# Differential values of all heads in 512-column products over four tiles of tokens, behind head 1's projections

## The chip, the cores and the metric

The kernel runs on one core of a Trainium2 chip. Five engines matter: TensorE (PE; its weight loads are shown apart as PEld) multiplies 128x128 blocks and writes only into PSUM; VectorE (DVE) and ScalarE (ACT) read PSUM and do the element work; GpSimd (POOL) does a few small steps and issues some transfers; SyncE (SP) issues most transfers. Each engine works through its own queue in order, and the engines wait for one another by semaphores. The metric is the device time of one execution in microseconds, the median of several.

## The reference

Two layers over 512 tokens of 1024 channels. Each layer normalises its input, projects it with one large matrix `w_in`, and feeds three token mixers (differential attention, a convolution module, neighbourhood attention), whose outputs are gated, merged and followed by a feed-forward block and a gated input embedding. The change touches the values of the differential attention, and one buffer of the neighbourhood attention:

```python
proj = h @ w_in[i]
qa, ka, va, glu_in, qc, kc, vc, gates = jnp.split(proj, SPLITS, axis=-1)
ya = diff_attention(qa, ka, va, ...)
...
v = va.reshape(B, S, HA, DV_A).transpose(0, 2, 1, 3)
...
a = jax.nn.softmax(s, axis=-1)
a = (a[:, :, 0] - lam * a[:, :, 1]).astype(v.dtype)
return jnp.einsum('bhqk,bhkd->bhqd', a, v)
```

There are four differential heads with values 128 wide, so `va` is 512 tokens by 512 columns. The neighbourhood attention has eight heads of 64, and its values `vc` are 512 by 512 too.

## The kernel before

Every operand of a product is split into a high and a low part, and a product is made of three matmuls (high by high, high by low, low by high) that add up in one PSUM bank. Activations lie with their channels on the partitions: `self.h` holds eight chunks of 128 channels by 512 tokens. A projection (`proj`, `gemm`) loads one block of weights of 128x1024, splits it on ACT and DVE, and makes 8 x 3 matmuls of 512 columns into a bank. `weights` issues the load and the split ahead of their place, by a priority; the loads go through SP's queue.

The order of TensorE's instructions is written by hand (`manual_schedule`): it is the order of the program text. The other engines' orders are laid out by a scheduler from priorities and readiness. PSUM has eight banks, handed out by tag: three "mm", two "sc", two "tr", one "av" (`pbufs`, line 297). A bank goes back to its tag when its last reader is done.

`layer` (line 428) lays out a layer: the convolution's gated input, the neighbourhood attention's projections of four pairs of heads (`natten_in`) and its values (`natten_v`), then the differential attention's projections of four heads (`diff_in`, each a query and a key) and its values, gates, output products and merging. Within this foreground the attention itself runs as units, generators that are put in a queue (`later`) with a delay and a gap: `chunk` counts the foreground's groups of matmuls, and every fourth call is a tick (`tick`), at which waiting units go on by one step and the next unit of the queue may start. So a unit's step stands at a fixed number of chunks, whatever the foreground then is.

A neighbourhood unit (`natten_unit`, line 695) takes two "sc" banks for its two 128x256 scores (`scores`, line 807; matmuls at L811), each read by one DVE operation that also takes a bias tile loaded from memory (load at L702, operation at L710); two ticks later it transposes the probabilities into "tr" banks, and two ticks after that it sums the values (L753, L754) into "av" for a pair's first head and into "mm" for its second (line 748). A differential unit (`diff_unit`, line 844) calls `probs` (line 892): twice a 128x512 score into an "sc" bank, a maximum on DVE (L902), and an exponential on ACT that reads the bank again (its instruction is recorded at the helper's line, L143). Every second unit goes on with transposes (L859) and value sums.

`diff_in` also takes the head's query and key through a rotation: a copy to "rp", four small transfers on SP's queue (L829), additions and products on DVE, a split, and small transfers that stack the parts (L660): four for the query, eight for the key.

`natten_v` (line 663) makes the neighbourhood values for all heads at once: four accumulators, one for each tile of 128 tokens, of 512 columns each (L676 to L678), in two "mm" banks, "av" and "sc". `diff_v` (line 840) makes the differential values in two calls for two heads each by `values` (line 599): two "mm" banks, each with two tiles of 256 columns (L615 to L619). The first call stands behind head 0's projections, the second behind head 2's. `_vblocks` lays out its weights. Both end in the split of the values on ACT and DVE.

## Time and profile before

| | |
|---|---|
| median of 3 runs | 1776.03 us |
| lowest and highest run | 1776.01 and 1777.37 us |
| span of the profiled execution | 1776.7 us |
| PE busy | 1767.5 us, 99% of the span |
| DVE busy | 1421.7 us, 80% |
| ACT busy | 894.4 us, 50% |
| POOL busy | 103.0 us, 6% |

The profile shows one execution; the runs give no other time for it than its span. A row of the timeline has its start in microseconds from the start of the span, the duration, the engine, the line of the kernel, the operation with what it writes and reads, and in brackets the idle time before it with the work that ended it. Matmuls overlap in the pipeline, so that the distance of two starts, not the duration, is what one costs. A row of waits has the engine and tile that waited, the one waited for, the microseconds in total, the count and the longest. A row of a stretch of time has the busy time and count of each engine in the order PE, PEld, DVE, ACT, POOL, then TensorE's granted clock (1.00 is full speed), the share of the transfer engines and GB/s.

### The profile page before, as it was taken

The page shows a single profiled execution, that of the slowest core. Times are in us where ns is not written, and L with a number is a line of the kernel's source. Part 1 is how long each engine was busy: PE and PEld are TensorE (multiplying, and loading weights), DVE is VectorE, ACT ScalarE, POOL GpSimd, SP SyncE. Part 2 cuts the span into 40 slices and gives each one's busy share as a digit, 9 for nine tenths or more (in the row PEclk, how much of TensorE's full clock was granted, in tenths as well). Part 3 has the DMA queues.
Part 4 walks back from the last instruction along what each step waited for, and adds up shares of the span by engine and source line. Part 5 has one row for each costly group of instructions (what it writes and reads, how often), then busy time and mean ns, then how long its engine had stood idle before and what let it go on. Part 6 is the DMA issues. An engine that isn't in the chain of part 4 may idle for free.

```text
span 1776.7 us, 27451 instructions
## 1 busy us (share of the span) xinstructions
PE 1767.5 (99%) x10210; PEld 1559.6 (88%) x10210; DVE 1421.7 (80%) x2418; ACT 894.4 (50%) x1561; POOL 103.0 (6%) x146
## 2 busy tenths in 40 slices
PE   9999999999999999999999999999999999999998
PEld 7888888888899899998888888888888998989987
DVE  7878887998798587787776788889887976867776
ACT  5577555225565254454545765452356643534454
POOL 0000000000111010100000000000001110101000
PEclk9999999999999999999999999999999999999999
DMA  5666641334757366543447655423357664655332
GB/s 202 188 186 176 161 125 42 113 98 140 230 150 193 109 167 160 132 131 123 145 124 198 176 165 149 113 71 95 93 179 198 171 179 115 173 144 151 98 108 92
DMA packets 113509, 256.07 MB, mean 144 GB/s; under 512 B 14560, under 2 KB 19424, under 8 KB 113376
## 3 DMA queue, kind: packets, MB, share of 16 engines
q1 hardware_dynamic: 99984, 229.93, 42.3%
q0 software_dynamic: 12672, 23.07, 8.3%
q8 instruction: 81, 1.33, 0.3%
q10 hardware_dynamic: 720, 1.31, 0.2%
q14 instruction: 52, 0.43, 0.1%
HBM read 215.46 MB, written 7.34 MB: 125 GB/s over the span
## 4 chain that ended last, share of the span: by engine, by line
PE 96%; DVE 2%; ACT 1%; issue 0%; DMA 0%; POOL 0%; ACTq 0%; POOLq 0%; DVEq 0%
PE ffn_mm L1017 4%; PE ffn_mm L1019 4%; PE ffn_mm L177 4%; PE ffn_mm L179 4%; PE ffn_mm L178 4%; PE ffn_mm L1018 4%; PE ffn_sc L1019 3%; PE ffn_sc L1017 3%; PE ffn_sc L1018 3%; PE mergea_mm L177 2%; PE mergea_mm L178 2%; PE mergea_mm L179 2%; PE diff_sc L811 2%; PE gatec_mm L177 2%; PE gatec_mm L178 2%; PE gatec_mm L179 2%
## 5 line engine op out<-in xcount | busy, mean ns | idle before, releaser
L160 DVE SCALAR_TENSOR_TENSOR conv_z<-glu_z,pre_par,conv_z 128x512 f32<-128x512 f32 x240 | 179.4, 748 | 3.3
L143 ACT ACTIVATE ffn_wh<-ffn_wr 128x1024 fp32r<-128x1024 f32 (+1 forms) x92 | 92.7, 1014 | 111.7 <-PE ffn_mm L178 77.1
L987 POOL DMA_DIRECT2D ffn_qk<-w_fu x88 | 78.0, 990 | 605.7 <-DMA ffn_qk<-w_fu 414.7
L157 DVE TENSOR_TENSOR ffn_wl<-ffn_wr,ffn_wh 128x1024 fp32r<-128x1024 f32 (+1 forms) x92 | 107.4, 1173 | 5.4 <-ACT ffn_wh L143 4.9
L157 DVE TENSOR_TENSOR ffn_t<-ffn_mm,wo_rb 128x512 f32<-128x512 f32 (+1 forms) x64 | 38.6, 604 | 67.9 <-PE ffn_mm L179 67.8
L143 ACT ACTIVATE mergea_wh<-mergea_wr 128x1024 fp32r<-128x1024 f32 (+1 forms) x32 | 27.1, 846 | 96.8 <-PE mergea_mm L178 79.6
L143 ACT ACTIVATE ffn_wh<-ffn_qk 128x1024 fp32r<-128x1024 f32 x44 | 46.7, 1060 | 35.9 <-PE ffn_mm L178 15.7
L157 DVE TENSOR_TENSOR ffn_wl<-ffn_qk,ffn_wh 128x1024 fp32r<-128x1024 f32 x44 | 53.8, 1224 | 11.3 <-ACT ffn_wh L143 11.3
L157 DVE TENSOR_TENSOR ffn_t<-ffn_t,ffn_t 128x512 f32<-128x512 f32 (+1 forms) x46 | 31.3, 680 | 31.4 <-ACT ffn_t L143 30.9
L143 ACT ACTIVATE diff_a<-diff_sc,diff_s 128x512 f32<-128x512 f32 x32 | 22.0, 686 | 61.0 <-DVE diff_s L902 61.0
L177 PE MATMUL ffn_mm<-ffn_v,ffn_wh 128*128 128x512 f32 x132 | 51.4, 389 | 0.0
L178 PE MATMUL ffn_mm<-ffn_v,ffn_wh 128*128 128x512 f32 x132 | 51.4, 389 | 0.0
L179 PE MATMUL ffn_mm<-ffn_v,ffn_wl 128*128 128x512 f32 x132 | 51.3, 389 | 0.0
L177 PE MATMUL ffn_mm<-ffn_y,ffn_wh 128*128 128x512 f32 x132 | 51.3, 389 | 0.0
L178 PE MATMUL ffn_mm<-ffn_y,ffn_wh 128*128 128x512 f32 x132 | 51.3, 389 | 0.0
L179 PE MATMUL ffn_mm<-ffn_y,ffn_wl 128*128 128x512 f32 x132 | 51.3, 389 | 0.0
L1019 PE MATMUL ffn_mm<-wo_h,ffn_wl 128*128 128x256 f32 x176 | 49.8, 283 | 0.0
L1019 PE MATMUL ffn_sc<-wo_h,ffn_wl 128*128 128x256 f32 x176 | 49.8, 283 | 0.0
L1018 PE MATMUL ffn_mm<-wo_h,ffn_wh 128*128 128x256 f32 x176 | 49.8, 283 | 0.0
L1018 PE MATMUL ffn_sc<-wo_h,ffn_wh 128*128 128x256 f32 x176 | 49.8, 283 | 0.0
L1017 PE MATMUL ffn_sc<-wo_h,ffn_wh 128*128 128x256 f32 x176 | 49.8, 283 | 0.0
L1017 PE MATMUL ffn_mm<-wo_h,ffn_wh 128*128 128x256 f32 x176 | 49.8, 283 | 0.0
(876 smaller groups left out, 6588.6 us busy)
## 6 DMA issues: line engine op xcount, KB each, us to landing
ffn_qk<-w_fu POOLq DMA_DIRECT2D x88, 256.0 KB, 5.7
ffn_wr<-w_fg SPq DMA_DIRECT2D x44, 512.0 KB, 3.7
ffn_wr<-w_fd SPq DMA_DIRECT2D x32, 448.0 KB, 3.9
ffn_r<-w_fu SPq DMA_DIRECT2D x44, 256.0 KB, 3.7
ffn_qk<-w_fg SPq DMA_DIRECT2D x44, 256.0 KB, 4.3
ffn_qk<-w_fu SPq DMA_DIRECT2D x44, 256.0 KB, 4.6
natten_wr<-w_in SPq DMA_DIRECT2D x16, 512.0 KB, 4.3
natten_b<-bias SPq DMA_DIRECT2D x32, 256.0 KB, 4.0
```

The lines of the kernel that those rows point to most:

```text
L143: i = self.nc.scalar.activation(out, in_, func, **kw)
L157: return self.nc.vector.tensor_tensor(out, a, b, op)
L160: return self.nc.vector.scalar_tensor_tensor(out, a, s, b, op0, op1)
L177: mm(out, wh, ah, start=first, stop=False)
L178: mm(out, wh, al, start=False, stop=False)
L179: mm(out, wl, ah, start=False, stop=last)
L811: self.nc.tensor.matmul(out, st4[:, u, qs], st[:, ks], start=n == 0, stop=n == 1)
L987: nc.gpsimd.dma_start(q, wu[:, lo], accum_op=ALU.add)
L1017: mm(out, wh[:, c], bh, start=first and k == 0, stop=False, skip_group_check=True)
L1018: mm(out, wh[:, c], bl, start=False, stop=False, skip_group_check=True)
L1019: mm(out, wl[:, c], bh, start=False, stop=k == 3, skip_group_check=True)
```

## The change

The wide loop of `natten_v` becomes a function of its own, `wide_values`, and the differential values use it: one call for all four heads, in 512-column products over four tiles of tokens, with the accumulators in the three "mm" banks and one "sc" bank. The call stands behind head 1's projections; the second call, behind head 2's, is gone. The neighbourhood sums of the last pair of heads take the "av" bank for both heads. The weights are laid out like the neighbourhood values'.

```diff
@@ layer
         self.diff_in(0, sd, ya)
-        self.diff_v(0, sd)
         self.diff_in(1, sd, ya)
+        self.diff_v(sd)
         self.gate_c(acc, 0)
         self.diff_in(2, sd, ya)
-        self.diff_v(1, sd)
         self.diff_in(3, sd, ya)
@@
-    def values(self, ap, parts):
+    def wide_values(self, ap, tags):
 
         mm = self.nc.tensor.matmul
-        accs = [self.ps("mm", (P, 2, 256)) for _ in range(2)]
-        for o in range(0, KD, 4):
-            wh, wl = self.weights(ap[:, o * 256:(o + 4) * 256], 1024)
...
+        accs = [self.ps(t) for t in tags]
+        for o in range(0, KD, 2):
+            wh, wl = self.weights(ap[:, o * 512:(o + 2) * 512], 1024)
+            self.background(self.low, self.bg["values"] if self.phase == "natten" else 0)
+            for k in (o, o + 1):
+                s = slice((k - o) * 512, (k - o + 1) * 512)
+                for t, out in enumerate(accs):
+                    hi, lo = (a[:, t * P:(t + 1) * P] for a in self.halves(self.h[k]))
+                    mm(out, hi, wh[:, s], start=k == 0, stop=False)
+                    mm(out, hi, wl[:, s], start=False, stop=False)
+                    mm(out, lo, wh[:, s], start=False, stop=k == KD - 1)
                     self.chunk()
...
+        return accs
@@ natten_v
-        accs = [self.ps(t) for t in ("mm", "mm", "av", "sc")]
...
+        accs = self.wide_values(self.a["w_vc"][self.i], ("mm", "mm", "av", "sc"))
@@ natten_unit
-        av = self.ps(("av", "mm")[u], (P, 256))
+        av = self.ps("av" if pr == 3 else ("av", "mm")[u], (P, 256))
@@
-    def diff_v(self, g, st):
+    def diff_v(self, st):
         self.phase = "diff"
-        st["v", g] = self.values(self.a["w_va"][self.i, g], lambda v, a: ((v[:, 0:256], v[:, 256:512], a),))
+        accs = self.wide_values(self.a["w_va"][self.i], ("mm", "mm", "mm", "sc"))
+        for g in range(2):
+            st["v", g] = [self.sb("v", [P, 2, 512], F32R) for _ in range(2)]
+            for t, acc in enumerate(accs):
+                v = st["v", g][t // 2][:, t % 2]
+                self.split(v[:, 0:256], v[:, 256:512], acc[:, g * 256:(g + 1) * 256])
@@ _layout
-        "w_va": _vblocks(w_in[:, :, OFF_VA:OFF_VA + 512]),
+        "w_va": _wide(w_in[:, :, OFF_VA:OFF_VA + 512]),
```

More of the change, by code (lines that the diff above doesn't have):

```diff
@@ L597, in conv @@
         yield from self.norm(st[0], CB, (3, 1), done)
-    def values(self, ap, parts):
+    def wide_values(self, ap, tags):
         mm = self.nc.tensor.matmul
-        accs = [self.ps("mm", (P, 2, 256)) for _ in range(2)]
-        for o in range(0, KD, 4):
-            wh, wl = self.weights(ap[:, o * 256:(o + 4) * 256], 1024)
-            both = [(k, t) for k in range(o, o + 4) for t in range(4)]
-            if o == 0:
-                both.sort(key=lambda kt: kt[1] // 2)
-            for n, (k, t) in enumerate(both):
-                s = slice((k - o) * 256, (k - o + 1) * 256)
-                out = accs[t // 2][:, t % 2, :]
-                ts = slice(t * P, (t + 1) * P)
-                mm(out, self.h[k][:, 0, ts], wh[:, s], start=k == 0 and t % 2 == 0,
-                   stop=False, skip_group_check=True)
-                mm(out, self.h[k][:, 0, ts], wl[:, s], start=False, stop=False,
-                   skip_group_check=True)
-                mm(out, self.h[k][:, 1, ts], wh[:, s], start=False,
-                   stop=k == KD - 1 and t % 2 == 1, skip_group_check=True)
-                if n % 2:
-                    self.chunk()
-        vs = []
-        for acc in accs:
-            v = self.sb("v", [P, 2, 512], F32R)
-            for t in range(2):
-                for hi, lo, a in parts(v[:, t], acc[:, t]):
-                    self.split(hi, lo, a)
-            vs.append(v)
-        return vs
+        accs = [self.ps(t) for t in tags]
[9 more added lines that the diff above has]
+                    mm(out, lo, wh[:, s], start=False, stop=k == KD - 1)
+                    self.chunk()
+        return accs
     def natten_in(self, pr, st, ys):
@@ L666, in natten_v @@
         self.phase = "natten"
-        mm = self.nc.tensor.matmul
-        accs = [self.ps(t) for t in ("mm", "mm", "av", "sc")]
-        for o in range(0, KD, 2):
-            wh, wl = self.weights(self.a["w_vc"][self.i][:, o * 512:(o + 2) * 512], 1024)
-            self.background(self.low, self.bg["values"])
-            for k in (o, o + 1):
-                s = slice((k - o) * 512, (k - o + 1) * 512)
-                for t, out in enumerate(accs):
-                    hi, lo = (a[:, t * P:(t + 1) * P] for a in self.halves(self.h[k]))
-                    mm(out, hi, wh[:, s], start=k == 0, stop=False)
-                    mm(out, hi, wl[:, s], start=False, stop=False)
-                    mm(out, lo, wh[:, s], start=False, stop=k == KD - 1)
-                    self.chunk()
+        accs = self.wide_values(self.a["w_vc"][self.i], ("mm", "mm", "av", "sc"))
         vs = [[self.sb("v", [P, 2, 512], F32R) for _ in range(2)] for _ in range(2)]
@@ L1359, in _blocks @@
     return np.ascontiguousarray(w).reshape(*lead, m // P, P, (k // P) * P)
-def _vblocks(w):
-    w = w.reshape(L, KD, P, 2, 256).transpose(0, 3, 2, 1, 4)
-    return np.ascontiguousarray(w).reshape(L, 2, P, KD * 256)
 def _wide(w):
```

## The prediction

> **What bounds the kernel now.** I read the busy line first, then the chain of waits, then the waits of TensorE, to see whether a TensorE microsecond is a microsecond of the kernel.

> ```profile
> PE 1767.5 (99%) x10210; PEld 1559.6 (88%) x10210; DVE 1421.7 (80%) x2418; ACT 894.4 (50%) x1561; POOL 103.0 (6%) x146
> PE 96%; DVE 2%; ACT 1%; issue 0%; DMA 0%; POOL 0%; ACTq 0%; POOLq 0%; DVEq 0%
> PE pre_av L325 <- DVE pre_zeror L398: 1.1, 1, 1.1
> PE natten_tr L734 <- ACT natten_e L143: 0.3, 2, 0.2
> PE natten_tr L736 <- ACT natten_e L143: 0.3, 2, 0.2
> PE natten_tr L736 <- DVE natten_a L157: 0.2, 1, 0.2
> ```

> PE is on 96% of the chain and waits for other engines 1.9 us in all. So the kernel is as long as PE's instruction stream: fewer PE cycles come off the span, and a new PE wait goes on it in full, since there is no idle time that it could replace. DVE and ACT have slack; what matters of them is how soon they empty a PSUM bank that PE wants.

> **The products themselves.** Per layer, `values` runs twice, 2 x 8 x 4 x 3 = 192 products of 256 columns; `wide_values` runs 8 x 4 x 3 = 96 of 512. Durations in the rows overlap, so the price is the distance of starts. First and last of 24 narrow ones, and of 9 wide ones (the neighbourhood values, the same loop):

> ```profile
> 198.72 0.28 PE L615 MATMUL diff_mm<-diff_wh,glu_h 128*128 128x256 f32 x1
> ...
> 201.48 0.28 PE L619 MATMUL diff_mm<-diff_wh,glu_h 128*128 128x256 f32 x1
> ```
> ```profile
> 70.20 0.39 PE L676 MATMUL natten_mm<-natten_wh,glu_h 128*128 128x512 f32 x1
> ...
> 72.02 0.39 PE L678 MATMUL natten_sc<-natten_wh,glu_h 128*128 128x512 f32 x1
> ```

> 2.76 / 23 = 0.120 us against 1.82 / 8 = 0.2275 us. Per layer 192 x 0.120 - 96 x 0.2275 = 23.0 - 21.8 = 1.2 us; two layers: **-2.4 us**. [...] Weight loads (4 of 1024 columns a layer), their splits and the eight evacuating splits keep their number and size: nothing.

> **What moves.** Both versions call the chunk counter 32 times a layer for these values, so the attention units, which start at fixed ticks (four chunks), keep their ticks while the projections around them change. Counting ticks from a layer's first neighbourhood projection: head 0 ends at 32 and head 1, now next, at 36; the values fill 36 to 44. The units there are: neighbourhood scores of the last unit (pair 3, second half, second head) at 37; neighbourhood sums of pair 3 at 38, 39, 40, 41; head 0's scores at 39, 41, 43 and 45. The rows of before fit this count: head 0's first scores come inside head 1's k projection, the second in gate_c, the third in head 2's q.

> During 36 to 44 the accumulators hold all three "mm" banks and one of the two "sc" banks. Every unit that asks for two "sc" banks now gets one, and PE, in order, stands until it is read. Behind the waiting matmul stand the remaining value products, gate_c and everything later; ACT and DVE then wait for those.

> **Head 0's scores.** `probs` makes two 128x512 scores (u = 0, 1). With one bank, u = 1 starts when the reduction and the exponential of u = 0 are done. First, second and third `probs` of layer 1:

> ```profile
> 172.32 0.48 PE L811 MATMUL diff_sc<-diff_qk 128*128 128x512 f32 x1
> 172.86 0.39 PE L811 MATMUL diff_sc<-diff_qk 128*128 128x512 f32 x1
> 174.31 1.28 DVE L902 TENSOR_REDUCE diff_s<-diff_sc 128x1 f32<-128x512 f32 x2
> 175.02 0.69 ACT L143 ACTIVATE diff_a<-diff_sc,diff_s 128x512 f32<-128x512 f32 x1 [1.80 <-DVE diff_s L902]
> ...
> 180.49 0.40 PE L811 MATMUL diff_sc<-diff_qk 128*128 128x512 f32 x1
> 182.73 0.69 ACT L143 ACTIVATE diff_a<-diff_sc,diff_s 128x512 f32<-128x512 f32 x1 [2.19 <-DVE diff_s L902]
> ...
> 186.88 0.39 PE L811 MATMUL diff_sc<-diff_qk 128*128 128x512 f32 x1
> 187.07 0.69 DVE L902 TENSOR_REDUCE diff_s<-diff_sc 128x1 f32<-128x512 f32 x1
> 187.86 0.69 ACT L143 ACTIVATE diff_a<-diff_sc,diff_s 128x512 f32<-128x512 f32 x1 [2.24 <-DVE diff_s L902]
> ```

> From the start u = 1 has now to the end of u = 0's exponential: 175.71 - 172.86 = 2.85, 183.42 - 180.49 = 2.93, 188.55 - 186.88 = 1.67 us. The third has DVE free at once (0.69 reduction, 0.69 exponential and the product's tail), so 1.67 is the floor. In the first two DVE first empties neighbourhood tiles, work that comes at the same ticks afterwards. Per layer from 3 x 1.67 = 5.0 to 2.85 + 2.93 + 1.67 = 7.5; I take 6.5, since the waiting itself lets DVE catch up somewhat: **+13.0 us** (10.0 to 15.0).

> [...]

> **The last neighbourhood scores.** Two 128x256 scores, each read by one DVE operation that also needs the bias tile:

> ```profile
> 163.68 0.36 PE L811 MATMUL natten_sc<-natten_qk 128*128 128x256 f32 x1
> ...
> 164.00 0.28 PE L811 MATMUL natten_sc<-natten_qk 128*128 128x256 f32 x1
> ```
> ```profile
> 164.60 1.85 SPq L702 DMA_DIRECT2D natten_b<-bias  x1
> ```
> ```profile
> 169.32 0.42 DVE L710 CUSTOM_DVE_ANT_0 natten_b<-natten_sc,natten_b 128x256 f32<-128x256 f32 x1
> ```

> The second score wants its bank at 164.00 and would get it at 169.74: 5.7 us, because this bias was issued late, behind the key and query stacks of head 0 on SP's queue. That is the upper bound. The lower is a bias already there: product tail (0.28) and DVE (0.42), 0.7 us. Head 1's 20 small transfers (8 rotations, 12 stacks) are moved forward on the same queue, but a bias is issued ahead by priority; between ends far apart I take the middle, 3.2 us: **+6.4 us** (1.4 to 11.4).

> **One "av" bank for four sums.** Sums of the second head used an "mm" bank:

> ```profile
> 167.47 0.23 PE L754 MATMUL natten_av<-natten_a,natten_x 128*128 128x128 f32 x1
> ...
> 170.84 0.64 PE L753 MATMUL natten_mm<-natten_pt,natten_v 128*128 128x256 f32 x4
> ```
> ```profile
> 171.13 0.42 DVE L157 TENSOR_TENSOR natten_y<-natten_y,natten_av 64x256 fp32r<-64x256 f32 x1
> ```

> The next sum starts at 170.84 and the bank would be free at 171.55: 0.7 us late, where DVE had been held by the bias above. Twice a layer, 0 to 0.7 each; I take 0.4 a layer: **+0.8 us** (0 to 2.8).

> **The ends of the values.** At the start the fourth accumulator takes an "sc" bank of the neighbourhood scores just before; nine products (2.05 us) cover it. At the end `gate_c` wants an "mm" bank and head 0's fourth scores the second "sc" bank. The same evacuation after the neighbourhood values ends with

> ```profile
> 76.69 0.41 DVE L157 TENSOR_TENSOR natten_v<-natten_sc,natten_v 128x256 fp32r<-128x256 f32 x1
> ```

> 77.10, or 5.1 us after the last product starts at 72.02. Until the fourth scores' u = 1 pass the product (0.23), eight transposes (0.8), twelve products of gate_c (2.7) and u = 0 (0.5), 4.2 us: 0.9 us short if DVE does that bank last. I take 0.6 a layer for both ends together: **+1.2 us** (0 to 3).

> **Sum.** -2.4 + 13.0 + 6.4 + 0.8 + 1.2 = +19.0 us on the profiled execution's span of 1776.7; its span lies 0.7 above the median of the runs, 1776.03, so **1795 us**. All low ends: -2.4 + 10.0 + 1.4 = +9.0, 1785.0. All high ends: -2.4 + 15.0 + 11.4 + 2.8 + 3.0 = +29.8, 1805.8.

> **Rivals.** *The banks come free in time (not slower).* Then only the shorter products are left: 1776.0 - 2.4 = 1773.6 us. It decides if the scores' bank is not held, that is if the units leave the ticks of the values. For it: bank waits on PE are absent from the table today. Against: at these ticks each unit takes two of two "sc" banks, and even the best row leaves 1.67 us.

> *Head 1's chain becomes the bound.* The rotary chains of heads 0 and 1 now follow each other with no values between. Their buffers ("rp", four) are held until the stacks are sent, and SP sends in order:

> ```profile
> 159.50 1.14 SPq L660 DMA_DIRECT2D diff_qk<-diff_kh  x2
> ...
> 163.26 1.24 SPq L660 DMA_DIRECT2D diff_x<-diff_rp  x2
> ```

> Head 0's k stacks end at 164.5, while head 1's k projection will end near 160 and wants one of these buffers to leave its "mm" bank. If it has to wait for them, the third accumulator waits some 4.5 us, twice: 1795 + 9 = 1804 us. Against: a rotated copy's buffer is freed earlier, by the addition.

> *The clock falls in the wait.* Near the end PE has no work after 1769.7:

> ```profile
> 1770.00:1774.00 4.00, 0.00 (x0) 0.00 (x0) 1.35 (x4) 0.71 (x2) 0.65 (x1) 1.00 0.66 244
> 1774.00:1774.50 0.50, 0.00 (x0) 0.00 (x0) 0.00 (x0) 0.00 (x0) 0.00 (x0) 1.00 0.41 143
> 1774.50:1775.00 0.50, 0.00 (x0) 0.00 (x0) 0.00 (x0) 0.00 (x0) 0.00 (x0) 0.73 0.06 20
> ```

> The granted clock stays 1.00 for about 5 us and then halves. Only a neighbourhood wait at its upper bound (5.7) is that long. At half clock for as long as the wait, PE loses 2.9 us a layer on top of the 5.7: 1795 + 2 x (5.7 - 3.2 + 2.9) = 1806 us. [...]

> **How the numbers follow.** Bank waits as summed: 0.80; banks free in time: 0.08; head 1's chain: 0.07; clock: 0.05. A measurement of this kernel can tell no less than about 0.2% (3.6 us) from no change, so 1773.6 would read as the same; faster needs 1.2 us more than the products give, 0.03. Same: 0.06, the rest of that rival and a little from partial waits. Slower: 0.91. The range reaches from 1784, just under all low ends, to 1806, all high ends and both slower rivals; left out are the first rival and small remainders.

> **What would show it.** Right: PE waits for ACT `diff_a` before three of L811's matmuls in each layer, 1.7 to 2.9 us each, and once for DVE L710; wide products 0.2275 us apart; PE's busy time down by about 2.4 us; no wait before the fourth scores above 1 us. Wrong: those three waits missing, or a largest wait at the first value products (head 1's chain), or a granted clock under 1.00 between the values. The prediction is wrong in size if the neighbourhood wait is outside 0.7 to 5.7 us, and wrong in kind if the span falls.

## The result and the profile after

| | before | after |
|---|---|---|
| median, lowest to highest | 1776.7 us, 1776.01 to 1778.1 (4 runs beside the changed kernel) | 1824.13 us, 1821.48 to 1825.63 (4 runs) |
| span of the profiled execution | 1776.7 us | 1823.0 us |
| PE busy, instructions | 1767.5 us, 10210 | 1779.3 us, 10018 |
| waits of PE for other engines, summed | 1.9 us | 38.1 us |
| mean granted clock of TensorE | 0.999 | 0.993 |

The ratio is 1.0265 (95% interval 1.0251 to 1.0280): slower by 47 us, where 19 were forecast and 30 was the upper end. The busy line of the page after, and the line of its chain by engine:

```profile
PE 1779.3 (98%) x10018; PEld 1554.1 (85%) x10018; DVE 1423.0 (78%) x2418; ACT 900.8 (49%) x1561; POOL 102.9 (6%) x146
PE 89%; DVE 5%; DMA 3%; ACT 2%; issue 1%; SPq 0%; POOL 0%; ACTq 0%; DVEq 0%; POOLq 0%
```

192 matmuls fewer, as counted, and yet 11.8 us more PE busy time: some matmuls must have become slower. PE's share of the chain falls from 96% to 89%; what it lost went to DVE, transfers and ACT. The table of PE's waits, which had four rows before (engine, line and tile that waited, the one waited for, microseconds, count, longest), now reads:

```profile
PE diff_sc L782 <- ACT diff_a L143: 10.1, 5, 2.8
PE natten_sc L782 <- DVE natten_s L681: 8.8, 2, 5.0
PE diff_mm L609 <- ACT diff_rp L143: 4.4, 2, 2.2
PE diff_tr L835 <- DVE diff_t L157: 3.2, 2, 1.6
PE diff_sc L782 <- DMA diff_qk<-diff_rp: 2.8, 1, 2.8
PE diff_sc L782 <- DVE diff_v L157: 2.4, 2, 1.2
...
PE natten_av L724 <- DVE natten_y L157: 1.3, 2, 0.7
...
PE gatec_mm L177 <- DVE diff_v L157: 0.9, 2, 0.4
```

(Lines 782, 609, 835 and 681 are the matmuls of the scores, of the wide products and of the differential transposes, and the reduction of the neighbourhood scores.) The waits are 36.2 us longer. The longest ones of layer 1 in order of time:

```profile
163.94 0.50 PE L609 MATMUL diff_mm<-diff_wh,glu_h 128*128 128x512 f32 x1 [2.21 <-ACT diff_rp L143]
...
171.35 0.58 PE L782 MATMUL natten_sc<-natten_qk 128*128 128x256 f32 x1 [3.87 <-DVE natten_s L681]
...
185.48 0.79 PE L782 MATMUL diff_sc<-diff_qk 128*128 128x512 f32 x1 [2.80 <-DMA diff_qk<-diff_rp]
197.12 0.50 PE L782 MATMUL diff_sc<-diff_qk 128*128 128x512 f32 x1 [2.01 <-ACT diff_a L143]
205.46 0.50 PE L782 MATMUL diff_sc<-diff_qk 128*128 128x512 f32 x1 [1.65 <-ACT diff_a L143]
```

The first is the first product of the third accumulator of the values: its "mm" bank still holds head 1's k projection. ACT's copy that frees it starts at 163.29, with no idle time of ACT from 158.81 up to it, and before the last stacks of head 0 are sent:

```profile
163.29 0.60 ACT L143 ACTIVATE diff_rp<-diff_mm 128x512 f32<-128x512 f32 x1
```
```profile
163.42 1.18 SPq L643 DMA_DIRECT2D diff_qk<-diff_rp  x2
```

The second is the last neighbourhood unit, the other three are head 0's first three `probs`, each waiting for its single "sc" bank. (At 185.48 the record names a transfer; the same matmul of layer 2 waits 2.80 us for ACT `diff_a`, and it is the bank here too: ACT's exponential of the first score runs from 184.65 to 185.34.)

The other part is the clock. The stretches of layer 2 around the neighbourhood wait, which there lasts from 1070.32 to 1075.29 (the granted clock is the number behind the five engines' busy times):

```profile
1073.00:1076.40 3.40, 1.11 (x4) 1.01 (x5) 0.71 (x3) 0.60 (x2) 0.00 (x0) 0.50 0.39 117
1076.40:1079.75 3.35, 3.35 (x10) 2.58 (x9) 2.55 (x7) 1.52 (x4) 0.00 (x0) 0.50 0.38 87
1079.75:1083.00 3.25, 3.25 (x21) 2.86 (x20) 1.67 (x3) 2.32 (x4) 0.00 (x0) 1.00 0.33 76
```

Half clock from 1073 on, while PE still waits, and through the next 4.5 us of work. In layer 1 the wide products show what it does to each:

```profile
172.37 0.63 PE L610 MATMUL diff_mm<-diff_wl,glu_h 128*128 128x512 f32 x1
172.80 0.63 PE L611 MATMUL diff_mm<-diff_wh,glu_h 128*128 128x512 f32 x1
...
191.66 0.40 PE L609 MATMUL diff_mm<-diff_wh,glu_h 128*128 128x512 f32 x1
191.89 0.39 PE L610 MATMUL diff_mm<-diff_wl,glu_h 128*128 128x512 f32 x1
```

0.43 us from start to start at half clock against 0.23 at full. The clock was at half from 165.00 to 175.24 and from 185.48 to 188.89 in layer 1, from 1072.94 to 1079.77 and from 1090.01 to 1093.42 in layer 2. Without the waits inside, PE worked 17.7 us there, and would have taken half of it at full clock: 8.8 us lost.

**The account** of the profiled execution: waits +36.2, clock +8.8, products -2.4 as priced, together +42.6; measured +46.3. The remaining 3.7 us over 23 new waits are 0.16 us each. An edge that the list leaves out has that size: idle time is counted from a matmul's modelled end (0.39 us after its start), while the next would have started 0.23 us after it. That it is this edge is not shown: in the place-alone kernel below the same sum leaves nothing over, and the spans of the kernel before differ by 2.7 us from execution to execution (1774.1 to 1776.8 us in thirteen later ones), the profiled one being among the longest.

### The profile page after: what moved, and what is told of

The parts are those of the page before. It is cut to its first block, busy times and chain, and to the rows that moved or that the text cites. A ratio compares the mean times of both kernels' runs of the same rounds, so it can differ in the third digit from the quotient of the medians.

```text
span 1823.0 us, 27073 instructions
## 1 busy us (share of the span) xinstructions
PE 1779.3 (98%) x10018; PEld 1554.1 (85%) x10018; DVE 1423.0 (78%) x2418; ACT 900.8 (49%) x1561; POOL 102.9 (6%) x146
## 4 chain that ended last, share of the span: by engine, by line
PE 89%; DVE 5%; DMA 3%; ACT 2%; issue 1%; SPq 0%; POOL 0%; ACTq 0%; DVEq 0%; POOLq 0%
PE ffn_mm L993 4%; PE ffn_mm L995 4%; PE ffn_mm L177 4%; PE ffn_mm L178 4%; PE ffn_mm L179 4%; PE ffn_mm L994 4%; PE ffn_sc L995 3%; PE ffn_sc L994 3%; PE ffn_sc L993 3%; PE mergea_mm L178 2%; PE mergea_mm L177 2%; PE mergea_mm L179 2%; PE gateb_mm L178 2%; PE gateb_mm L177 2%; PE wo_mm L177 2%; PE gateb_mm L179 2%
## 5 line engine op out<-in xcount | busy, mean ns | idle before, releaser
L143 ACT ACTIVATE ffn_wh<-ffn_wr 128x1024 fp32r<-128x1024 f32 (+1 forms) x92 | 92.8, 1015 | 111.9 <-PE ffn_mm L178 79.0
L157 DVE TENSOR_TENSOR ffn_wl<-ffn_wr,ffn_wh 128x1024 fp32r<-128x1024 f32 (+1 forms) x92 | 107.4, 1173 | 5.6 <-ACT ffn_wh L143 5.0
L157 DVE TENSOR_TENSOR ffn_t<-ffn_mm,wo_rb 128x512 f32<-128x512 f32 (+1 forms) x64 | 38.7, 605 | 68.1 <-PE ffn_mm L179 68.1
L143 ACT ACTIVATE mergea_wh<-mergea_wr 128x1024 fp32r<-128x1024 f32 (+1 forms) x32 | 27.1, 848 | 96.8 <-PE mergea_mm L178 79.4
L878 DVE TENSOR_REDUCE diff_s<-diff_sc 128x1 f32<-128x512 f32 x64 | 43.2, 687 | 29.3 <-PE diff_sc L782 29.2
L143 ACT ACTIVATE ffn_wh<-ffn_qk 128x1024 fp32r<-128x1024 f32 x44 | 46.7, 1061 | 36.6 <-PE ffn_mm L178 15.9
L157 DVE TENSOR_TENSOR ffn_wl<-ffn_qk,ffn_wh 128x1024 fp32r<-128x1024 f32 x44 | 53.8, 1224 | 10.7 <-ACT ffn_wh L143 10.7
L157 DVE TENSOR_TENSOR ffn_t<-ffn_t,ffn_t 128x512 f32<-128x512 f32 (+1 forms) x46 | 31.3, 680 | 31.9 <-ACT ffn_t L143 31.4
```

What stands on the lines that cost most here:

```text
L143: i = self.nc.scalar.activation(out, in_, func, **kw)
L157: return self.nc.vector.tensor_tensor(out, a, b, op)
L878: nc.vector.tensor_reduce(out=m[:, u:u + 1], in_=sc, op=ALU.max, axis=AX.X, negate=True)
```

## The experiments

The ratios are against runs of the kernel before on the same chip. A kernel without a ratio was timed in a single execution, beside 1777.05 us of the kernel before; what its trace shows carries it.

### Which part costs it: place, banks, width

*Width.* The changed kernel, with every 512-column product of the differential values made as two of 256:

```diff
-                    mm(out, hi, wh[:, s], start=k == 0, stop=False)
...
+                    for g in range(1 if self.phase == "natten" else 2):
...
+                        mm(out[:, q], hi, wh[:, c], start=k == g == 0, stop=False, skip_group_check=True)
```

> The changed kernel with its place and its four accumulators, but products of 256 columns (two for each of 512). If the loss is all in the banks and the place: the changed kernel's 1824 us and 2.4 us more, 1824 to 1829 us, the same waits of L782, and 2.4 us more of product time. If the wide products themselves bring on part of the loss (longer groups, later evacuation): below 1820 us.

1827.03 us, ratio 1.0282 (1.0267 to 1.0298). The loss stays; the products' share is 2.9 us by the medians, near the forecast 2.4, though the two kernels' intervals overlap and their waits differ too (36.8 us in sum here, 38.1 in the changed kernel).

*Place.* The kernel before, with both its narrow calls behind head 1, in two "mm" banks as ever:

```diff
         self.diff_in(0, sd, ya)
-        self.diff_v(0, sd)
         self.diff_in(1, sd, ya)
+        self.diff_v(0, sd)
+        self.diff_v(1, sd)
         self.gate_c(acc, 0)
         self.diff_in(2, sd, ya)
-        self.diff_v(1, sd)
         self.diff_in(3, sd, ya)
```

> The kernel before with its narrow products, but both calls behind head 1's projections; each call holds two mm banks and no sc bank. Theory of bank waits: the place alone costs only the later start of heads 2 and 3 (the wait of the transposes, L859 here, for a tr bank, 3.2 us in the changed kernel) and small change, 1778 to 1783 us; no wait of L811 for diff_a, no fall of the clock. Rival (the rotation chains of heads 0 and 1 side by side are the loss): waits of PE for diff_rp and diff_qk as in the changed kernel and 1790 us or more.

1799.59 us, ratio 1.0127 (1.0112 to 1.0142), with no accumulator in an "sc" bank and the sums' banks untouched: 23 us for the place alone. The time is the rival's, but not by the waits that it named: PE's waits in this kernel are 17.5 us, none of them for a copy to `diff_rp`, and none for a bank of head 0's scores:

```profile
PE natten_tr L734 <- DVE natten_pt L157: 6.2, 2, 3.1
PE natten_sc L811 <- DVE natten_s L710: 4.4, 4, 1.2
PE diff_tr L859 <- DVE diff_t L157: 3.2, 2, 1.6
```

The first of them in DVE's timeline, and the matmul that it lets go:

```profile
173.81 0.69 DVE L157 TENSOR_TENSOR diff_rp<-diff_rp,diff_kh 128x512 fp32r<-128x512 f32 x1
...
176.21 0.68 DVE L157 TENSOR_TENSOR diff_rp<-diff_rp,diff_r 128x512 f32<-128x512 f32 x1
176.92 0.69 DVE L157 TENSOR_TENSOR natten_pt<-natten_tr,natten_pt 128x512 fp32r<-128x512 f32 x1
```
```profile
177.76 0.30 PE L734 MATMUL natten_tr<-pre_ident,natten_e 128*128 128x128 f32 x1 [3.10 <-DVE natten_pt L157]
```

DVE never stands idle between these rows. It works through head 1's rotation, and the operation that empties the transposes' bank has its turn behind it. In the kernel before, the values stood between the two heads' projections and gave PE work while DVE rotated. With 15.6 us more waits and three falls of the clock (by the reckoning above 4.9 us) the sum is 20.5 us, and this span is 20.3 us longer. So the 47 us go, along these steps, to the place (1776.5 to 1799.6), to the four held banks and the sums' single bank (1799.6 to 1827.0, 27 us), less the 3 of the wider products.

*One "av" bank alone.* The kernel before with only that edit:

```diff
-        av = self.ps(("av", "mm")[u], (P, 256))
+        av = self.ps("av" if pr == 3 else ("av", "mm")[u], (P, 256))
```

> The kernel before with one edit alone: the neighbourhood sums of the last pair of heads take the av bank for both heads. The prediction's term: two waits of PE a layer of 0 to 0.7 us for the bank, 0 to 2.8 us in all, 1776.5 to 1779.5 us; the waits of natten_av for natten_y were 1.3 us in the changed kernel. If the edit matters more there: over 1780 us.

1779.46 us, ratio 1.0016 (1.0006 to 1.0025). Two waits a layer, where the prediction had counted the bank as late by 0.7 us twice at most:

```profile
171.08 0.71 PE L753 MATMUL natten_av<-natten_pt,natten_v 128*128 128x256 f32 x4 [0.70 <-ACT natten_e L143]
180.23 0.71 PE L753 MATMUL natten_av<-natten_pt,natten_v 128*128 128x256 f32 x4 [0.79 <-DVE natten_y L157]
```

PE's waits rise from 1.9 to 4.7 us and the time by 2.9 us: these short waits cost their length, and the mean clock stayed at 1.00. The price was right at its upper end.

### Which units pay, and can they be moved out of the way

*Head 0's scores behind the values.* In the changed kernel head 0's units start five ticks later:

```diff
-            self.later(self.diff_unit(head, qt, st4, k2, st, box, ys), 6 if head else 7, 2)
+            self.later(self.diff_unit(head, qt, st4, k2, st, box, ys), 6 if head else 12, 2)
```

> The changed kernel, with head 0's units starting 12 ticks after its projections instead of 7, so that none of its scores stands between the value products; the last neighbourhood scores and sums still do. Theory (waits for a bank, each followed by a spell of half clock): the waits of L782 for diff_a (12.9 us with the one put down to a transfer), the two for the second score bank (2.4 us) and the second fall of the clock in each layer (3.2 us of half clock each, 1.6 us of time) are gone: about 1824 - 12.9 - 2.4 - 3.2 = 1805 us, with the neighbourhood wait (3.9 and 5.0 us) and the first fall unchanged. Rival (ACT, DVE and SP are late because the chains of heads 0 and 1 follow each other, and PE waits for them somewhere anyway): the waits turn up at other places, 1815 us or more.

1843.8 us. The scores' waits fell from 12.9 to 3.5 us, so the held "sc" bank was their cause. But the total rose by 20:

```profile
PE diff_tr L227 <- DVE diff_pt L157: 16.7, 4, 6.1
...
PE diff_tr L227 <- POOL diff_rc L223: 6.8, 2, 3.4
```

The late units now hold "tr" banks that the normalisations need. The waits for the held bank can't be had back this way; of the total it says only that the rival's time, 1815 us or more, came.

*The values behind the first gate product*, so that head 1's chain has that much more time, and head 0's units two ticks later:

```diff
-        self.diff_v(sd)
         self.gate_c(acc, 0)
+        self.diff_v(sd)
...
-            self.later(self.diff_unit(head, qt, st4, k2, st, box, ys), 6 if head else 7, 2)
+            self.later(self.diff_unit(head, qt, st4, k2, st, box, ys), 6 if head else 9, 2)
```

> The changed kernel, with the values one gate projection later (two ticks) and head 0's units two ticks later too, so that three of its scores still fall between the value products, but the last neighbourhood scores and head 1's last copy do not. Theory of bank waits: the neighbourhood wait (8.8 us), the wait for head 1's copy (4.4 us) and the first fall of the clock (about 5 us of time in both layers) are gone, the scores' waits of 10 to 13 us stay: about 1824 - 18 = 1806 us. Rival (the chains of heads 0 and 1 are late): the gate's bank or the scores wait for them instead, 1815 us or more.

1829.26 us. The neighbourhood's wait for its scores and the wait for `diff_rp` are gone, and one of 10 us a layer has come; here it is with the transfers and the work of DVE and ACT ahead of it:

```profile
174.43 2.72 SPq L800 DMA_DIRECT2D diff_rp<-diff_rp  x4
```
```profile
179.99 0.69 DVE L157 TENSOR_TENSOR diff_rp<-diff_rp,diff_r 128x512 f32<-128x512 f32 x1 [3.71 <-DMA diff_rp<-diff_rp]
```
```profile
182.70 0.63 ACT L143 ACTIVATE diff_kh<-diff_rp 128x512 fp32r<-128x512 f32 x1 [5.48 <-DVE diff_rp L157]
183.24 0.58 ACT L143 ACTIVATE gatec_x<-gatec_mm 128x512 f32<-128x512 f32 x1
```
```profile
183.87 0.79 PE L609 MATMUL diff_mm<-diff_wh,glu_h 128*128 128x512 f32 x1 [10.01 <-ACT gatec_x L143]
```

The gate's bank was ready to be read, but ACT, in order, stood 5.5 us at head 1's split for DVE; DVE had stood 3.7 us for the rotated parts, whose transfers left SP's queue only from 174.43. Head 1's chain is late whoever comes next.

*A bias buffer from another set for the last neighbourhood unit*, so that its load need not wait for an earlier unit's tile:

```diff
-        b = self.sb("b", [P, 2, NW])
+        b = self.sb("t" if (pr, half, u) == (3, 1, 1) else "b", [P, 2, NW])
```

> The changed kernel, with the bias of the last neighbourhood unit in a buffer of its own, so that its load need not wait for an earlier unit. If the long neighbourhood wait is the bias transfer: it shrinks from 3.9 and 5.0 us to 0.7 to 1.2 us each, and the clock is half for a shorter time after it, about 1824 - 7 - 3 = 1814 us. If it is DVE's own backlog: it stays above 3 us and the time at 1822 to 1826 us.

1819.3 us, between the two forecasts. The neighbourhood wait fell from 8.8 to 3.9 us and that for `diff_rp` from 4.4 to 2.1; 3.3 us came up for `natten_e`, and the scores' stayed at 12.9. The bias was about half of that wait; the other half is the shared bank with DVE's queue ahead of it. PE's waits shrank by 6.0 us in sum, the span by 5.5 (the changed kernel's own four spans differ by 4.1).

*The neighbourhood's tail and heads 2 and 3's units one tick earlier*, in the place-alone kernel and in the changed one:

```diff
-            self.later(self.natten_unit(pr, n // 2, n % 2, st4, k2, st, ys[pr]), 6 if pr == 3 else 5 if pr else 10, 1)
+            self.later(self.natten_unit(pr, n // 2, n % 2, st4, k2, st, ys[pr]), 4 if pr == 3 else 5 if pr else 10, 1)
...
-            self.later(self.diff_unit(head, qt, st4, k2, st, box, ys), 6 if head else 7, 2)
+            self.later(self.diff_unit(head, qt, st4, k2, st, box, ys), (7, 6, 5, 5)[head], 2)
```

> The kernel before with both narrow calls behind head 1 (1799.6 us without further edits), and pair 3's neighbourhood units due four instead of six ticks behind their pair (the queue lets them start one tick earlier), heads 2 and 3's units five instead of six. If the place costs time because the tail of the neighbourhood meets head 1's rotary chain on VectorE and SyncE: the waits for natten_s and natten_pt (12 us), for diff_t (3.2) and the three clock falls (about 5) go for the most part, 1780 to 1788 us. If two chains side by side cost that wherever the units stand: 1793 or more.

> The changed kernel (1824.1 us) with the same earlier units. If the waits add: the neighbourhood scores' 8.8 us and diff_t's 3.2 go, the 12.9 of head 0's scores and the 4.4 for diff_rp stay, and a fall of the clock a layer stays: 1807 to 1813 us. If the waits only change places (VectorE as late elsewhere): 1817 or more.

1800.82 us, ratio 1.0133 (1.0116 to 1.0150), with the place alone, and 1821.11 us, ratio 1.0251 (1.0236 to 1.0266), in the changed kernel. In the first, PE's waits add up to 17.6 us as against 17.5: those for `natten_pt` fell from 6.2 to 4.7, those for `natten_s` came to 4.7 after 4.4, and 4.1 us for `diff_v` are new. The rival's time came, 1793 us or more. Only the wait for `diff_t` was cured (3.2 us, with 1.2 for `diff_pt` in its place); it had come because heads 2 and 3's units stand a tick later since the move. In the second the sum fell by 5 us, and the time is again the one forecast for waits that change places, 1817 us or more. What an earlier unit meets, in DVE's timeline of that kernel and PE's row that it ends:

```profile
147.49 0.69 DVE L157 TENSOR_TENSOR diff_rp<-diff_rp,diff_r 128x512 f32<-128x512 f32 x1
...
149.48 0.42 DVE L157 TENSOR_TENSOR natten_y<-natten_y,natten_mm 64x256 fp32r<-64x256 f32 x1
149.93 0.69 DVE L157 TENSOR_TENSOR diff_rp<-diff_rp,diff_rp 128x512 f32<-128x512 f32 x1
...
152.16 0.42 DVE L681 CUSTOM_DVE_ANT_0 natten_b<-natten_sc,natten_b 128x256 f32<-128x256 f32 x1
```
```profile
152.64 0.39 PE L782 MATMUL natten_sc<-natten_qk 128*128 128x256 f32 x1 [2.91 <-DVE natten_s L681]
```

DVE is never idle between these rows: the unit that came too late for head 1's chain now stands behind head 0's.

*Two passes.* The wide products with two "mm" banks at a time, two tiles of tokens behind head 0 and two behind head 1; the weights are loaded and split twice, no "sc" bank is held, the sums keep their two banks, and heads 2 and 3's units stand a tick earlier:

```diff
         self.diff_in(0, sd, ya)
+        self.diff_v(0, sd)
         self.diff_in(1, sd, ya)
-        self.diff_v(sd)
+        self.diff_v(1, sd)
...
-        accs = self.wide_values(self.a["w_va"][self.i], ("mm", "mm", "mm", "sc"))
+        accs = self.wide_values(self.a["w_va"][self.i], ("mm", "mm"), 2 * h)
```

> Wide products in two mm banks at a time: tiles 0 and 1 of the tokens behind head 0, tiles 2 and 3 behind head 1, all heads in both, with the value weights loaded and split twice (four more loads of 512 KB, ACT 1.06 and DVE 1.22 us each, a layer); the sc banks, the third mm bank and the av bank as before, and heads 2 and 3 start their units one tick earlier than the changed kernel's. If the banks were the loss: no wait of L811's matmuls for diff_a, no fall of the clock, and 1774 to 1780 us, the product gain of 2.4 less what DVE's extra 9.8 us cost where it is already 88% busy. If wide products or the chains cost by themselves: 1785 us or more.

> The values in two passes of wide products, one behind each head (1786.6 us), with pair 3's units one tick earlier. If the neighbourhood's waits of 4.9 us there come from meeting the values: 1780 to 1783 us. If they move along with the units: 1785 to 1789. Faster than the kernel before (under 1774) only if all waits but those of before go and the products' 2.4 us are all that is left.

1786.62 us, ratio 1.0053 (1.0037 to 1.0070); with the neighbourhood's tail a tick earlier 1812.85 us, ratio 1.0203 (1.0188 to 1.0218). With nothing held and the heads apart, 37 of the 47 us are back, which confirms banks and place from the other side. The time forecast for banks alone, 1774 to 1780 us, did not come: it is still 10 us behind the kernel before, with 7.8 us more waits, in ten kinds of at most 2.1 us, and a clock that stays at 0.999. Their sum less the products' 2.4 leaves 4.2 us of the span, which the edges of some 16 waits don't quite fill; that part stays open, and so does what the second load and split of the weights, which only this kernel has, add to the waits. The tick earlier, meant to free 4.9 us, missed both its forecasts: it brought waits of 3.9 (for `natten_s`), 3.8 (`diff_a`) and 3.1 us (`diff_v`), and six falls of the clock. No variant beat the kernel before. The width alone is worth 2.4 to 2.9 us, so that such a version could save about 0.15%.

### When the clock falls

To measure it by itself, the kernel before with 40 pauses of TensorE of graded length in the feed-forward block (each a chain of 1 to 10 copies on ACT between two small matmuls; four of the 44 places get no copy and no pause):

```diff
+        self.pause(fb % 11)
...
+        mm(ps, self.ones_r, self.zero_r, start=True, stop=True)
...
+            for k in range(n):
+                self.act(o, ps if k == 0 else o, AF.Copy)
+        ps = self.ps("tr", (P, P))
+        mm(ps, self.zero_r, o, start=True, stop=True)
```

> The kernel before, with 44 pauses of TensorE added in the feed-forward blocks, of 0 to 10 small ACT copies each, to see after which length of a pause the granted clock falls. By the row at the end of the kernel before (the clock halves some 5 us after the last matmul): no fall for pauses under 5 us. By the changed kernel (a fall after a wait of 2.2 us, none after 2.0 and 1.65): falls from about 2.2 us on, half clock for some 3.2 us, a loss of about 1.6 us each on top of the pause.

1917.4 us, mean clock 0.974. Neither 5 us nor a fixed length fits: the longest of the 40 pauses was 3.5 us, and two of the same 1.79 us went different ways. Here they are, with the stretches behind them:

```profile
554.94 0.33 PE L1078 MATMUL ffn_tr<-pre_probe,pre_zeror 128*128 128x128 f32 x1 [1.79 <-ACT pre_probe L143]
...
1505.64 0.33 PE L1078 MATMUL ffn_tr<-pre_probe,pre_zeror 128*128 128x128 f32 x1 [1.79 <-ACT pre_probe L143]
```
```profile
554.94:556.40 1.46, 1.46 (x12) 1.46 (x13) 1.46 (x5) 0.28 (x1) 1.15 (x2) 1.00 0.00 0
556.40:557.40 1.00, 1.00 (x7) 1.00 (x7) 1.00 (x2) 0.39 (x1) 0.61 (x1) 0.53 0.41 70
```
```profile
1507.00:1509.00 2.00, 2.00 (x19) 2.00 (x18) 1.25 (x3) 0.61 (x2) 0.79 (x1) 1.00 0.57 100
```

The first fell, 1.5 us after PE had gone back to work; the second did not, and neither did one of 2.81 us before 827.23. What sorts them is a grid: starts of half clock within one execution lie whole multiples of 3.41 us apart (in the changed kernel 165.00 and 185.48, six of them, and 1072.94, 266; in the place-alone kernel 157.70 and 178.18, six, and 1069.06, 267). The traces of the kernels before and after from end to end, the attention of five others, and the places shown here and below of this kernel and the place-alone one, cut at these points, agree: a stretch at full clock with 1.79 us or more of idle time was followed by one at half clock (1.79 here, 553.05 to 556.46), and one with up to 1.69 us was not (in the two passes with the tail a tick earlier, 148.33 to 151.74). The pauses of 1.79 and 2.81 us that passed were each cut in two by a point of the grid (1505.37 and 826.11), the first into 1.5 and 0.3 us, the second into 1.7 and 1.1.

Two places of the place-alone kernel show it without any pause made for the purpose. The same two waits stand in layer 1 and in layer 2:

```profile
156.00 0.39 PE L811 MATMUL natten_sc<-natten_qk 128*128 128x256 f32 x1 [1.20 <-DVE natten_s L710]
157.51 0.44 PE L811 MATMUL natten_sc<-natten_qk 128*128 128x256 f32 x1 [1.01 <-DVE natten_s L710]
...
1047.84 0.39 PE L811 MATMUL natten_sc<-natten_qk 128*128 128x256 f32 x1 [1.19 <-DVE natten_s L710]
1049.35 0.39 PE L811 MATMUL natten_sc<-natten_qk 128*128 128x256 f32 x1 [1.01 <-DVE natten_s L710]
```
```profile
157.75:161.00 3.25, 3.25 (x10) 2.57 (x10) 0.73 (x6) 2.74 (x9) 0.00 (x0) 0.50 0.89 238
...
1048.70:1052.00 3.30, 2.65 (x13) 2.24 (x14) 1.55 (x9) 2.50 (x8) 0.00 (x0) 1.00 0.87 259
```

In layer 1 both lie between two points of the grid (154.29 and 157.70), 2.2 us together, and the clock falls. In layer 2 a point (1048.6, six steps ahead of the next fall at 1069.1) parts them into 1.4 and 0.8 us, and it stays. So idle time added up within a stretch; no single long wait was needed, the longest here being 1.20 us.

To stay at half took less idle time than to fall. Of the stretches at half clock in the same traces, those with 0.64 us of idle time or more were followed by another (0.64 from 185.88 on in the changed kernel with the narrow products), those with up to 0.40 us were not (0.40 from 178.18 on in the place-alone kernel). So the changed kernel's first fall lasts three steps, 165.00 to 175.24: the first has 0.93 us of idle time, the second 2.93, and only the third is busy throughout.

## Why the prediction was wrong

The direction and the likeliest mechanism were right, the time was 18 us above the range. By its own steps:

- **Products, -2.4:** right. 0.23 us from start to start at full clock, as priced; the medians of two kernels are 2.9 us apart, with intervals that overlap.
- **Head 0's scores, +13.0:** 12.9 us (10.1 and the 2.8 put down to a transfer), in six waits of 2.80, 2.0 and 1.65 us, twice each, of the three `probs` that were named. The two from rows whose DVE work came again lay near the row (2.8 for 2.85) or below it (2.0 for 2.93), the third at its floor.
- **Last neighbourhood scores, +6.4 (1.4 to 11.4):** 8.8 us, within. That a bias would be issued ahead by priority did not save it: it was issued at 166.61, behind head 0's stacks again, and the run with a buffer from another set gave half of the wait back.
- **One "av" bank, +0.8 (0 to 2.8):** 1.3 us here, 2.9 alone.
- **Ends of the values, +1.2 (0 to 3):** 3.3 us (2.4 and 0.9), just above the upper end. The fourth scores wait 1.2 us a layer, over the 1 us that the prediction allowed them, the gate 0.4.
- **The step that failed** is the one that put what the place costs beside the sum instead of in it. "Head 1's chain becomes the bound" got 0.07 as a case of its own, on the argument that "a rotated copy's buffer is freed earlier, by the addition". The wait came, 2.2 us a layer at the very matmul that was named (the third accumulator's first), at half the price, and on top of the held banks, but not by a held buffer: the copy ran before head 0's last stacks were sent, so the argument held, and what it stood behind was the work in ACT's queue (four neighbourhood exponentials, two copies out of the transposes' banks, head 0's last split and a split of weights). It is also only the smallest sign of what the place costs: with nothing held, the move alone costs 23 us, since DVE and ACT go through the two heads' rotations in order, and the neighbourhood's bank is emptied behind them. The prediction had followed every unit's tick and asked which bank it finds, but not what stands ahead of its operations on DVE and ACT once the values no longer part the two chains. The 3.2 us for `diff_t` belong here too: only head 0's units had been followed, not those of heads 2 and 3.
- **The clock** got 0.05, from the end of the profile, where it stayed at 1.00 for 5 us. That row gave a delay for one position of the grid, not the idle time that is needed: with the fall at 1774.73, the grid point before lies at 1771.32 with 1.65 us of idle time in the stretch ahead of it, after which the clock stayed at 1.00. Four falls came and cost 8.8 us, only one of them from the neighbourhood wait: the first of layer 1 follows the 2.21 us of the third accumulator, and the second of each layer the 2.80 us of the first scores. Each came after a stretch with 2.2 to 2.8 us of idle time (2.21, 2.80, 2.78 and 2.80), which the waits made, so this was a consequence of the forecast's own waits and no rival to it.
- **From span to time:** the prediction took 0.7 us off, since the profiled span lay above the median of the runs. The profiled execution of the kernel before was a long one; wherever a span and its time are both on record (1823.0 and 1824.81 us for the changed kernel), the time is the longer by 1.7 to 3.0 us. The slip is small beside the miss.

So of the 46.3 us of the profiled execution, the prediction's own terms hold 23.9 (-2.4 + 12.9 + 8.8 + 1.3 + 3.3) against 19.0 forecast; 9.9 are further waits (4.4, 3.2, and 2.3 net in small ones), 8.8 from the clock, and 3.7 the rest. Two cases listed as alternatives, the clock and the wait at the third accumulator, happened together with the likeliest.

## What to carry to other kernels

When foreground work is moved, ask not only which banks and buffers the units at each tick will find, but what it parted: two chains on DVE and ACT that ran under it may now follow each other, and what empties a bank may come behind them (here with 3.10 us of PE's time in one such wait). Ask of each rival whether it excludes the forecast or adds to it; those that follow from it belong in the sum. And where TensorE begins to wait some 2 us at a time, as here, count a fall of the clock to each wait that can't be told to fall short: an estimated 1.7 us of work lost, half of a step of 3.41 us, and more where PE waits again within it (3.2 us in the three steps from 165.00 on in the changed kernel).
